# Attention's value products with 32 columns of weights, placed behind the scan's products by the list scheduler

## The chip, the cores and the metric

The kernel runs on one core of one Trainium2 chip. The metric is the device time of one execution in microseconds (us), as the median of several executions. Lower is better.

## The reference

One layer of a streaming encoder, 512 frames of 1024 columns, float32. Two token mixers work on the same input and are merged by gates. The change lies where the two mixers are computed side by side: the scan of the one (a delta rule) and the softmax attention of the other.

```python
x = x + 0.5 * swiglu(rms_norm(x, ffn1_norm), ffn1_w1, ffn1_w3, ffn1_w2)
h = rms_norm(x, mix_norm);  p = h @ w_in
# mixer A, 8 heads of 64, one step per frame
sa = einsum('bhvk,bhk->bhv', state, a_t)
state = state * w_t + sa * b_t^T + v_t * k_t^T
y_t = einsum('bhvk,bhk->bhv', state, r_t)
# mixer B, 8 heads of 64, blocks of 128 queries
s = einsum('bhqd,bhkd->bhqk', q_i, k) * scale + c_i[:, None] - cum[None, :]   # masked: s <= t
o = einsum('bhqk,bhkd->bhqd', softmax(s), v)                                  # "the values"
x = x + (sigmoid(g_A) * y_A + sigmoid(g_B) * y_B) @ w_out
x = x + 0.5 * swiglu(rms_norm(x, ffn2_norm), ffn2_w1, ffn2_w3, ffn2_w2)
out = rms_norm(x, final_norm)
```

## The kernel before, in words

Almost all matrix products are done three times over with split operands (a high and a low part), in a full 128x128 array. They fill the time before and after the stage that matters here.

In the stage of the change the kernel cuts the 512 frames into 16 chunks of 32 for the scan. One chunk is a chain over three engines: `product_x` (TensorE, tile `xps`), `copy_x` (VectorE, `Xs`), `product_u` (TensorE, `ups`), `copy_u` (ScalarE, into `RD`), `products_sy` (TensorE, `sps` for the state and `yps` for the output), `scale_s` (VectorE, back into `RD`), and then the next chunk's `product_x`. The products of `xps`, `sps` and `yps` use 32 columns of weights each, at one of four places (columns 0, 32, 64, 96 of the array). Those of `ups` use 64 rows and 64 columns, at one of two places. Before every second chunk `stage` transposes values (`vp`) and keys (`bp`), and every fourth chunk ends in transposes `yt`.

Around this chain the attention of four pairs of heads is computed (`Pair`, and `Block` for one or two blocks of 128 queries of a pair: three such objects for each pair, twelve in all). A `Block` makes its logits (`lp<-kb,qa` and `lp<-klc,qb`, full array), their maxima (VectorE), exponentials (ScalarE, tile `pts`) and division (VectorE), transposes them (`lp<-ident,pts`, full array), copies them to `tr` (ScalarE), and multiplies the values with them in `values` (`lp<-tr,vt`). In the kernel before, `values` uses 64 columns of weights for each of the two heads of a pair, at columns 0 and 64.

What is left of the time on TensorE is filled with columns of the input projection (`pq`, `pgt`: full array, 512 columns at a time, one third of a step being one instruction).

The order is made by a list scheduler, the class `Plan`, when the program is built. Every operation is entered by `op` with an engine, an estimated duration, what it depends on, a rank (SCAN before SIDE, NEXT, ROWS, FILL), buffers that it takes and frees (`takes`, `frees`: `tr` and `pf` are those of the attention's transposed weights and of its PSUM banks) and, on TensorE, a kind: `w` full-array products, `t` transposes, `m` products of 32 columns, `u` those of `ups`, and in the kernel before `n` for the values. `start` says when an operation could begin: after its dependencies, plus a margin (`lag`, `ahead`). `run` takes the operation that can begin first; of several, the one with the longest way behind it, with a bonus for a transposition behind `m`, `n` or `u`. `SWITCH` adds a price for a change of kind. The engines' queues then run in that order, each strictly in turn; whoever is not ready makes the rest of its queue wait. The queues of SyncE and GpSimd (loads and saves) are put in order by the framework.

Of the kernel before, what the change touches and what calls it, by code (L numbers as in the profile page):

```python
# [18 lines left out]
P = 128  # L19
# [6 lines left out]
NP = DA // P  # L26
C = 32
# [23 lines left out]
def kernel(  # L51
# [24 lines left out]
    dve, act, pe = [Queued(e, False) for e in (nc.vector, nc.scalar, nc.tensor)]  # L76
# [95 lines left out]
    SCAN, SIDE, NEXT, ROWS, FILL = range(5)  # L172

    def on(do, *a):
        return lambda: do(*a)

    class Plan:
# [9 lines left out]
        def op(s, engine, us, do, *deps, rank=0, takes=(), frees=(), later=0.0, kind="w"):  # L187
            s.ops.append(dict(engine=engine, us=us, do=do, deps=deps, rank=rank, takes=takes, frees=frees, later=later,
                              kind=kind, end=None, way=0.0))
            return s.ops[-1]  # L190

        def start(s, o):
            to, now = o["engine"], s.idle.get(o["engine"], 0.0)
            ahead = 0.0 if to != "PE" else 0.57 if o["rank"] == SCAN else 0.26 if o["rank"] == SIDE and o["kind"] in "tw" else 0.31
            for d in o["deps"]:
                if d["end"] is None:
                    return None
                by = d["engine"]
                lag = 0.32 if by == "PE" else 0.15 if by == to else 0.21
                now = max(now, d["end"] + (0.0 if by == to == "PE" else lag + ahead))  # L200
            for name in set(o["takes"]):
                n = sum(t == name for t in o["takes"])
                if len(s.room[name]) < n:
                    return None
                now = max(now, sorted(s.room[name])[n - 1])
            return now

        def run(s):
            todo = list(s.ops)
            for o in s.ops[::-1]:  # L210
                o["way"] = o["way"] + o["us"] if o["rank"] != FILL else 0.0
                for d in o["deps"]:
                    d["way"] = max(d["way"], o["way"] + 0.3)
            while todo:
                at = {n: now for n, o in enumerate(todo) for now in [s.start(o)] if now is not None}

                def first(n):
                    o = todo[n]
                    turn = o["engine"] == "PE" and o["kind"] == "t" and s.kind in "mnu"
                    return at[n], -o["way"] - (40.0 if turn else 0.0), n  # L220

                n = min(at, key=first)
                o = todo[n]
                if o["engine"] in ("DVE", "ACT") and o["rank"] != SCAN:
                    until = at[n] + 0.98 * o["us"]
                    n = next((m for m in at if todo[m]["engine"] == o["engine"] and todo[m]["rank"] == SCAN
                              and at[m] < until), n)
                o = todo.pop(n)
                us = o["us"]
                if o["engine"] == "PE":  # L230
                    change = "".join("n" if k in "mnu" else k for k in (s.kind, o["kind"]))
                    us += s.SWITCH.get(change, 0.0) if s.kind != o["kind"] else 0.0
                    s.kind = o["kind"]
                s.idle[o["engine"]] = at[n] + us
                o["end"] = at[n] + us + o["later"]
                for name in o["takes"]:
                    s.room[name].remove(min(s.room[name]))
                for name in o["frees"]:
                    s.room[name].append(o["end"] + 0.33)
                if o["do"]:  # L240
                    o["do"]()

# [810 lines left out]
    op = o1.enter_context(tc.tile_pool(name="o1", bufs=1, side="right"))  # L1053
# [37 lines left out]
    with ExitStack() as mx:  # L1091
# [284 lines left out]
        for t in range(C - 1):  # L1376
            n, m = t + 1, C - 1 - t
# [4 lines left out]
        tw = nc.scalar.dma_start(Td[:], TT)  # L1382
        Tb = Tall[:].rearrange("p (a c t) -> p a c t", a=2, c=NC)
        tv = Td[:].rearrange("(q i u) s t -> q i s u t", q=2, i=2)
        for i in range(2):
            for q in range(2):
                o = i * 64 + q * C
# [3 lines left out]
        def heads():  # L1391
            return [(p, q) for p in range(NP) for q in range(2)]

        def half(q):
            return slice(q * 64, (q + 1) * 64)
# [54 lines left out]
        vt = []  # L1450
# [8 lines left out]
        for b in range(NB):  # L1459
            o = vtp.tile([P, T], F32, name=f"vt{b}", tag=f"vt{b}")  # L1460
# [19 lines left out]
        at = b1.go(range(2))  # L1480
# [9 lines left out]
        at = b1.go(range(2, 5), a0.sum(at))  # L1490
        a1.out()
        b0.high()
        ahead = Gate(NP + 2)
        at = b1.go(range(5, 7), b0.sum(at))
# [5 lines left out]
        for q in range(2):  # L1500
            o = (1 - q) * 64
# [9 lines left out]
        at = ahead.go(range(7))  # L1511
        gate_out, ahead = ahead.out, ahead.go(range(7, KD), b1.sum(at))
        for q in range(2):
            o = (1 - q) * 64
# [7 lines left out]
        for q in range(2):  # L1522
            pool.memset(Rs[0][half(q), :, q, :], 0.0)
            for i in range(4):
                o = (1 - q) * 64
# [5 lines left out]
        op = plan.op  # L1531
        summed, gone = [op("SP", 0.0, None, later=us, frees=frees) for us, frees in ((3.0, ()), (3.5, ["w"]))]
        o = op("ACT", 0.69, b1.log, summed, rank=SCAN, takes=["t"], frees=["pf"])
        o = op("ACT", 0.63, b1.root, o, rank=SCAN)
# [33 lines left out]

        def product_x(c):
            Y["x"] = xps = pr.tile([P, 2, 64], F32, tag="b", name="xps")  # L1570
            for p, q in heads()[::-1]:
                o = (p // 2) * 64 + q * C
                pe.matmul(xps[o:o + C, p % 2, :], G[p][q][:, c, 0, :], Rs[c % 4][:, p, q, :], start=True, stop=True,
                          tile_position=(0, o))
# [4 lines left out]

        def product_u(c):  # L1580
            Y["u"] = ups = pr.tile([P, 2, 64], F32, tag="b", name="ups")
            for p in range(NP):
                h = half(p // 2)
                pe.matmul(ups[h, p % 2, :], Tb[h, p % 2, c, :], Y["Xs"][h, p % 2, :], start=True, stop=True)

# [135 lines left out]
        for m in range(NP + 3, 2 * KD):  # L1721
            g = Held()
            w, o = columns("pgt", COL_GA + m * P)
# [11 lines left out]
            o = op("DVE", 0.61, result, o, rank=NEXT, takes=["gs"], frees=["pm"])  # L1735
            if m + 1 < 2 * KD:
                o = op("ACT", 0.54 if tanhs else 1.82, opened, o, *roots, rank=ROWS)
# [47 lines left out]
        class Block:  # L1785
# [46 lines left out]
            def values(s):  # L1832
                for j, b in enumerate(s.bl):
                    for k in range(b + 1):
                        o = s.at[b] + k * P
                        for q in range(2):
                            h = 2 * s.pair.p + q
                            pe.matmul(s.lp[1][half(q), j * P:(j + 1) * P], vt[k][:, h * 64:(h + 1) * 64],
                                      s.tr[q][:, o:o + P], start=k == 0, stop=k == b)

            def copy_o(s):
                dve.tensor_copy(s.pair.qp[:, s.bl[0] * P:(s.bl[-1] + 1) * P], s.lp[1][:, 0:len(s.bl) * P])
# [1 line left out]
            def enter(s, operands):  # L1844
                for q in range(2):
                    us = sum(0.455 * (b + 1) * P / T + 0.02 for b in s.bl)
                    sees.append(op("PE", us, on(s.logits, q), *operands[q], rank=SIDE, takes=["pf"]))
                lit = sees[-2:]
                for q in range(2):
                    o = []  # L1850
                    for b in s.bl:
                        n = (b + 1) * P
                        e = op("DVE", 0.18 + 1.05e-3 * n, on(s.maximum, q, b), lit[q], rank=SIDE)
                        o.append(op("ACT", 0.26 + 0.83e-3 * n, on(s.exp, q, b), e, *turned[q][-1:], rank=SIDE))
                    exps.extend(o)
                    us = 0.16 + sum(0.13 + 0.69e-3 * (b + 1) * P for b in s.bl)
                    o = op("DVE", us, on(s.divide, q), *o, rank=SIDE)
                    lit[q] = op("PE", 0.11 * s.w / P, on(s.turn, q), o, rank=SIDE, kind="t")
                for q in range(2):
                    turned[q].append(lit[q])  # L1860
                o = [op("ACT", 0.1 + 0.75e-3 * s.w, on(s.copy_t, q), lit[q], *copies[-1:], rank=SIDE, takes=["tr"],
                        frees=["pf"] * (1 - q)) for q in range(2)]
                copies.append(o[1])
                us = 0.22 * sum(b + 1 for b in s.bl)
                o = op("PE", us, s.values, *o, rank=SIDE, frees=["tr"] * 2, kind="n")
                return op("DVE", 0.13 + 0.55e-3 * len(s.bl) * P, s.copy_o, o, rank=SIDE, frees=["pf"])

        outs = []
# [19 lines left out]
        o = []  # L1888
        for p in range(NP):
            o = op("ACT", 0.63, on(part_y, p), *outs[p], *sees, *o, rank=FILL)  # L1890
            o = [op("DVE", 0.69, on(part_l, p), o, rank=FILL)]
# [292 lines left out]
```

## Time and profile before

| | |
|---|---|
| runs shown | 1098.98, 1097.88, 1099.1 us; median 1098.98 us |
| profiled execution | 1097.66 us, of which the profile's span covers 1095.8 us |
| granted TensorE clock | 0.998 |
| TensorE busy | 99% of the span |
| VectorE, ScalarE, GpSimd busy | 76%, 61%, 19% |
| stage with the scan and the attention | from about 516 to 649 us of the span |

Times of lines are the start in us from the beginning of the span and the duration in us. A line joins instructions of one form that follow each other (x12). A matmul's own duration includes its way through the array, so several overlap; the distance from one line's start to the next line's start is what it holds the queue for. A float32 product stands as two records, a float32r product or a transposition as one.

### The profile page before, as it was taken

The numbers are of one execution on the slowest core, as the hardware profiler recorded it, in microseconds if no ns is written. First come the engines' busy times: TensorE is split into PE (matmuls) and PEld (weight loads), VectorE is DVE, ScalarE is ACT, GpSimd is POOL, SyncE is SP. The second block draws the span as 40 slices with busy tenths as digits, with TensorE's granted clock in tenths as the row PEclk, the third lists the DMA queues.
The fourth block names the chain that finished last, engine by engine and source line by source line (L and its number), as shares of the span: only waits on it lengthen the run. The fifth ranks groups of instructions, "written<-read, shape, count | busy, mean of one in ns | idle before, by whom it ended". The sixth has DMA issues, their size and how long they took to land.

```text
span 1095.8 us, 16697 instructions
## 1 busy us (share of the span) xinstructions
PE 1087.1 (99%) x6306; PEld 887.4 (81%) x6306; DVE 837.8 (76%) x1162; ACT 670.1 (61%) x1050; POOL 212.5 (19%) x255
## 2 busy tenths in 40 slices
PE   9999999999999999999999999999999999999997
PEld 7888888888887888888777777888888888888886
DVE  7997676789756699788877766877697766689874
ACT  6765556575554755346988856534576565576554
POOL 1211220134204112401000030112311202114210
PEclk9999999999999999999999999999999999999999
DMA  7989887879936434444112252645968888859972
GB/s 225 250 174 235 198 178 202 192 143 191 231 98 184 114 94 128 114 136 116 50 41 84 81 200 88 189 118 172 271 153 192 189 215 174 184 158 203 236 187 77
DMA packets 139725, 177.11 MB, mean 162 GB/s; under 512 B 9726, under 2 KB 75838, under 8 KB 139646
## 3 DMA queue, kind: packets, MB, share of 16 engines
q0 software_dynamic: 33328, 70.40, 33.7%
q1 hardware_dynamic: 105582, 104.21, 31.1%
q10 hardware_dynamic: 736, 1.45, 0.3%
q8 instruction: 50, 0.82, 0.3%
q14 instruction: 29, 0.24, 0.1%
HBM read 163.51 MB, written 12.52 MB: 161 GB/s over the span
## 4 chain that ended last, share of the span: by engine, by line
PE 97%; ACT 2%; DVE 1%; issue 0%; DVEq 0%; ACTq 0%
PE P L71 39%; PE P L145 5%; PE P L144 5%; PE P L143 5%; PE pgt L71 5%; PE lp L71 3%; PE pq L71 2%; PE ppj L71 2%; PE pk L145 2%; PE pk L143 2%; PE pk L144 2%; PE pb L71 2%; PE pa L71 1%; PE pw L144 1%; PE pw L145 1%; PE pw L143 1%
## 5 line engine op out<-in xcount | busy, mean ns | idle before, releaser
L71 PE MATMUL P<-sraw,q 128*128 128x512 f32 x344 | 91.3, 389 | 0.0
L135 ACT CAST whi<-raw 128x1024 fp32r<-128x1024 f32 (+3 forms) x43 | 41.1, 956 | 65.8 <-issue 19.3
L71 PEld LDWEIGHTS P<-sraw,q 128*128 128x128 f32 x344 | 64.6, 188 | 13.4
L71 PE MATMUL P<-swhi,q 128*128 128x512 f32 x224 | 71.4, 390 | 0.0
L71 PE MATMUL P<-sraw,wxh 128*128 128x512 f32 x200 | 68.4, 394 | 0.0
L136 DVE TENSOR_TENSOR wlo<-raw,whi 128x1024 fp32r<-128x1024 f32 (+3 forms) x44 | 49.6, 1127 | 16.3 <-ACT whi L135 15.2
L71 PE MATMUL P<-swhi,wxh 128*128 128x512 f32 x144 | 56.9, 395 | 0.0
L71 PE MATMUL P<-swhi,wxl 128*128 128x512 f32 x144 | 56.1, 390 | 0.0
L71 PE MATMUL P<-swlo,wxh 128*128 128x512 f32 x144 | 56.1, 389 | 0.0
L704 POOL DMA_DIRECT2D cb<-in_ffn_w_dram x20 | 24.1, 1204 | 150.1 <-DVE cd L71 85.3
L71 PE MATMUL P<-sraw,wxl 128*128 128x512 f32 x136 | 53.0, 390 | 0.0
L704 POOL DMA_DIRECT2D cd<-in_ffn_w_dram x24 | 29.5, 1229 | 102.6 <-DVE swlo L71 38.7
L71 PEld LDWEIGHTS P<-swhi,q 128*128 128x128 f32 x224 | 42.0, 188 | 8.7
L71 PE MATMUL P<-swlo,q 128*128 128x512 f32 x112 | 43.6, 389 | 0.0
L71 PEld LDWEIGHTS P<-sraw,wxh 128*128 128x128 f32 x200 | 37.2, 188 | 7.3
L71 ACT CAST sraw<-cd 128x1024 fp32r<-128x1024 f32 x30 | 31.5, 1050 | 15.1 <-PE P L71 11.5
L71 DVE TENSOR_TENSOR swlo<-ca,swhi 128x1024 fp32r<-128x1024 f32 x24 | 29.2, 1222 | 14.0 <-ACT swhi L71 14.0
L71 DVE TENSOR_TENSOR swlo<-cc,swhi 128x1024 fp32r<-128x1024 f32 x20 | 24.5, 1224 | 19.0 <-ACT swhi L71 18.7
L71 DVE TENSOR_TENSOR u<-P,u 128x512 f32<-128x512 f32 x52 | 34.1, 684 | 5.8 <-ACT u L71 5.7
L563 POOL DMA_DIRECT2D ca<-in_ffn_w_dram x16 | 19.3, 1205 | 96.2 <-DVE swlo L71 66.4
L143 PE MATMUL pk<-xh,whi 128*128 128x512 f32 x96 | 37.8, 394 | 0.0
L145 PE MATMUL pk<-xh,wlo 128*128 128x512 f32 x96 | 37.5, 391 | 0.2 <-DVE wlo L136 0.2
(616 smaller groups left out, 3446.9 us busy)
## 6 DMA issues: line engine op xcount, KB each, us to landing
raw<-in_w_in_dram SPq DMA_DIRECT2D x40, 512.0 KB
cc<-in_ffn_w_dram SPq DMA_DIRECT2D x36, 512.0 KB
cb<-in_ffn_w_dram POOLq DMA_DIRECT2D x36, 512.0 KB, 6.1
cb<-in_ffn_w_dram SPq DMA_DIRECT2D x32, 512.0 KB
cd<-in_ffn_w_dram POOLq DMA_DIRECT2D x32, 512.0 KB, 7.5
ca<-in_ffn_w_dram POOLq DMA_DIRECT2D x32, 512.0 KB, 7.6
ca<-in_ffn_w_dram SPq DMA_DIRECT2D x20, 512.0 KB
cd<-in_ffn_w_dram SPq DMA_DIRECT2D x18, 512.0 KB
```

Source lines behind the costliest of these rows:

```text
L71: q.last = do(*a, **kw)
L135: (hi_eng or act).copy(hi[:], raw[:])
L136: (eng or dve).tensor_tensor(lo[:], raw[:], hi[:].bitcast(F32), op=ALU.subtract)
L143: pe.matmul(ps, whi, xhi, start=first, stop=False, skip_group_check=onto)
L144: pe.matmul(ps, whi, xlo, start=False, stop=False, skip_group_check=onto)
L145: return pe.matmul(ps, wlo, xhi, start=False, stop=last, skip_group_check=onto)
L563: nc.gpsimd.dma_start(s.sum[g], src, accum_op=ALU.add)
L704: nc.gpsimd.dma_start(to, s.block(b, n, h), accum_op=ALU.add)
```

## The change

`values` now uses 32 columns of weights for each product, so four products take the place of two, at columns 0, 32, 64 and 96, each with the same 128 columns of moving operand as before. Its kind becomes `m`, like the scan's products. In the scheduler a value block that is not put behind a product of kind `m` is held back by 1.61 us more, and one that can follow such a product gets a bonus of 200 over the others that could begin at the same time. Margins and the bonus for transpositions get other numbers. `product_x` goes round four places instead of two by two, and `product_u` alternates between its two places.

```diff
-            ahead = 0.0 if to != "PE" else 0.57 if o["rank"] == SCAN else 0.26 if o["rank"] == SIDE and o["kind"] in "tw" else 0.31
+            ahead = 0.0 if to != "PE" else 0.75 if o["rank"] == SCAN else 0.27 if o["rank"] == SIDE else 0.36
+            ahead += 1.61 if o["kind"] == "m" != s.kind and o["rank"] != SCAN else 0.0
...
-                lag = 0.32 if by == "PE" else 0.15 if by == to else 0.21
+                lag = 0.28 if by == "PE" else 0.15 if by == to else 0.15
...
-                    turn = o["engine"] == "PE" and o["kind"] == "t" and s.kind in "mnu"
-                    return at[n], -o["way"] - (40.0 if turn else 0.0), n
+                    turn = o["engine"] == "PE" and o["kind"] == "t" and s.kind in "mu"
+                    same = o["kind"] == s.kind == "m"
+                    return at[n], -o["way"] - (10.0 if turn else 200.0 if same else 0.0), n
...
-                    until = at[n] + 0.98 * o["us"]
+                    until = at[n] + 1.11 * o["us"]
...
-                    s.room[name].append(o["end"] + 0.33)
+                    s.room[name].append(o["end"] + 0.35)
...
-            for p, q in heads()[::-1]:
+            for p, q in ((3, 1), (1, 1), (3, 0), (1, 0), (2, 1), (0, 1), (2, 0), (0, 0)):
...
-            for p in range(NP):
+            for p in (0, 2, 1, 3):
...
-                        for q in range(2):
-                            h = 2 * s.pair.p + q
-                            pe.matmul(s.lp[1][half(q), j * P:(j + 1) * P], vt[k][:, h * 64:(h + 1) * 64],
-                                      s.tr[q][:, o:o + P], start=k == 0, stop=k == b)
+                        for m in range(0, P, C):
+                            h = s.pair.p * P + m
+                            pe.matmul(s.lp[1][m:m + C, j * P:(j + 1) * P], vt[k][:, h:h + C],
+                                      s.tr[m // 64][:, o:o + P], start=k == 0, stop=k == b, tile_position=(0, m))
...
-                o = op("PE", us, s.values, *o, rank=SIDE, frees=["tr"] * 2, kind="n")
+                o = op("PE", us, s.values, *o, rank=SIDE, frees=["tr"] * 2, kind="m")
```

The order on TensorE, first place: the second value block (`lp<-tr,vt`), near the end of the fourth chunk, in the kernel before. `yps` ends the chunk's scan products, `pq` is filling work, `yt` are the transpositions of the scan's output.

```order
L71 MATMUL yps<-RD_4157,G_2539 32x64
L71 MATMUL pq<-xh_2444,whi 128x512
L71 MATMUL pq<-xl_2445,whi 128x512
L71 MATMUL pq<-xh_2444,wlo 128x512
L71 MATMUL lp<-tr,vt_3853 64x128 x2
L71 MATMUL lp<-tr,vt_3855 64x128 x2
L71 MATMUL lp<-tr,vt_3857 64x128 x2
L71 MATMUL yt<-ident,BK_2546 128x128
```

The same block on TensorE in the changed kernel.

```order
L71 MATMUL yps<-RD_4157,G_2539 32x64
L71 MATMUL lp<-tr,vt_3853 32x128 x4
L71 MATMUL lp<-tr,vt_3855 32x128 x4
L71 MATMUL lp<-tr,vt_3857 32x128 x4
L71 MATMUL lp<-ident,pts 128x128 x8
L71 MATMUL yt<-ident,BK_2546 128x128
```

The filling work between the scan's products and the values is gone from here; it stands elsewhere in the queue. The values are twice as many products of half the columns.

Second place, TensorE from the second chunk's `yps` to the third chunk's `ups`, in the kernel before. `lp<-ident,pts` transposes the weights of one head, `lp<-kb` and `lp<-klc` are logits of a later block.

```order
L71 MATMUL yps<-RD_4156,G_2539 32x64
L71 MATMUL pq<-xh_2593,whi 128x512
...
L71 MATMUL lp<-ident,pts 128x128 x3
...
L71 MATMUL xps<-RD_4157,G_2538 32x64
L71 MATMUL lp<-kb_4206,qa_4258 128x384
L71 MATMUL lp<-klc_3934,qb_4184 128x384
L71 MATMUL lp<-tr,vt_3853 64x128 x4
L71 MATMUL lp<-tr,vt_3855 64x128 x2
L71 MATMUL ups<-Xs,Tall 64x64 x4
```

The same stretch in the changed kernel.

```order
L71 MATMUL yps<-RD_4156,G_2539 32x64
L71 MATMUL lp<-ident,pts 128x128 x3
L71 MATMUL pq<-xh_2593,whi 128x512
...
L71 MATMUL lp<-kb_4206,qa_4261 128x384
L71 MATMUL lp<-klc_3934,qb_4184 128x384
...
L71 MATMUL xps<-RD_4157,G_2538 32x64
L71 MATMUL lp<-tr,vt_3853 32x128 x8
L71 MATMUL lp<-tr,vt_3855 32x128 x4
L71 MATMUL pq<-xh_2444,whi 128x512
...
L71 MATMUL ups<-Xs,Tall 64x64 x4
```

The values moved up to stand directly behind `xps`, the transpositions moved up to stand directly behind `yps` (three filling products less between them), and the logits moved ahead of `xps`.

Third place, SyncE's queue of loads at the end of the stage, in the kernel before. `G<-bsave` and `G<-lgsave` overwrite tiles that the scan's last `yps` read; `raw` are weights.

```order
L128 DMA raw<-in_w_in_dram 128x8x128 x4
L128 DMA raw<-in_fox_proj_dram 128x4x128
L1917 DMA G_2544<-bsave 128x512
L1915 DMA G_2543<-lgsave 96x512
L1917 DMA G_2545<-bsave 128x512
L128 DMA raw<-in_fox_proj_dram 128x4x128 x7
```

The same in the changed kernel.

```order
L128 DMA raw<-in_w_in_dram 128x8x128 x3
L128 DMA raw<-in_fox_proj_dram 128x4x128 x2
L1919 DMA G_2544<-bsave 128x512
L1917 DMA G_2543<-lgsave 96x512
L1919 DMA G_2545<-bsave 128x512
L128 DMA raw<-in_fox_proj_dram 128x4x128 x6
```

One load of weights has moved ahead of an earlier group of such loads, and one more stands before the three that wait for the scan.

Over the stage the twelve value blocks stand on TensorE so. Before: two between full-array products on both sides (the third and the twelfth), four between such products and transpositions (the second, fifth, ninth and tenth), six with a scan product (`xps`, `sps` or `ups`) directly before or behind them. After: eleven directly before or behind products of kind `m`, one (the third) between full-array products. The number of filling products, logits and transpositions is the same; 48 filling products stand behind the last `yt`, where 63 stood.

More of the change, by code (lines that the diff above doesn't have):

```diff
@@ L230, in run @@
                 if o["engine"] == "PE":
-                    change = "".join("n" if k in "mnu" else k for k in (s.kind, o["kind"]))
+                    change = "".join("n" if k in "mu" else k for k in (s.kind, o["kind"]))
                     us += s.SWITCH.get(change, 0.0) if s.kind != o["kind"] else 0.0
```

## The prediction

> **What bounds the kernel now.** I read the page's first part and its chain first, to see which engine sets the end.
>
> ```profile
> span 1095.8 us, 16697 instructions
> PE 1087.1 (99%) x6306; PEld 887.4 (81%) x6306; DVE 837.8 (76%) x1162; ACT 670.1 (61%) x1050; POOL 212.5 (19%) x255
> PE 97%; ACT 2%; DVE 1%; issue 0%; DVEq 0%; ACTq 0%
> ```
>
> TensorE (PE) is busy for 99% of the span and is 97% of the chain that ended last. Next, the busy time by stretches, with the stage of the change (516 to 649 us) and the tail behind it.
>
> ```profile
> 516.00:649.00 133.00, 132.44 (x1762) 99.71 (x1761) 101.18 (x256) 110.29 (x291) 9.78 (x18) 1.00 0.27 79
> 649.00:663.00 14.00, 14.00 (x65) 11.64 (x63) 2.61 (x3) 5.28 (x7) 3.20 (x7) 1.00 0.73 232
> ```
>
> The first number behind the length is PE: 132.44 of 133.00 us, at a granted clock of 1.00. VectorE (101.18) and ScalarE (110.29) have a quarter and a sixth of the stage to spare. The view of waits, for PE in this stage, has two entries alone:
>
> ```profile
> PE bp L71 <- ACT BK L71: 0.3, 1, 0.3
> PE lp L71 <- ACT tr L71: 0.3, 1, 0.3
> ```
>
> So the scan's chain over three engines does not set the pace. PE does, by what its queue holds: filling work covers the chain's latencies, and some of it is left over behind the scan. A microsecond taken from PE's queue here is a microsecond off the end, unless a wait takes its place. What can be taken is not arithmetic (the same columns stream through the array) but what a change of the array's shape costs. That cost is not shown as idle time; it is in the distances between starts.
>
> **The price of a change of shape.** The timeline of PE around the second and the third value block:
>
> ```profile
> 546.46 0.39 PE L71 MATMUL pq<-xh,wlo 128*128 128x512 f32 x1
> 546.77 0.65 PE L71 MATMUL sps<-RD,RD 128*32 128x64 f32 x32
> 547.25 0.41 PE L71 MATMUL yps<-RD,G 128*32 128x64 f32 x16
> 547.58 0.50 PE L71 MATMUL pq<-xh,whi 128*128 128x512 f32 x1
> 547.92 0.40 PE L71 MATMUL pq<-xl,whi 128*128 128x512 f32 x1
> 548.16 0.40 PE L71 MATMUL pq<-xh,wlo 128*128 128x512 f32 x1
> 548.49 0.88 PE L71 MATMUL lp<-tr,vt 128*64 128x128 f32 x12
> 549.29 0.66 PE L71 MATMUL yt<-ident,BK 128*128 128x128 f32 x4
> ...
> 553.48 1.09 PE L71 MATMUL lp<-tr,vt 128*64 128x128 f32 x16
> 554.50 0.50 PE L71 MATMUL pq<-xh,whi 128*128 128x512 f32 x1
> 554.84 0.40 PE L71 MATMUL pq<-xl,whi 128*128 128x512 f32 x1
> ```
>
> A value block of 12 records holds PE for 549.29 - 548.49 = 0.80 us, one of 16 for 554.50 - 553.48 = 1.02. Four records are 0.22, so one is 0.055 and the streams themselves are 0.66 and 0.88; the remaining 0.15 of each block is getting into and out of its shape. The neighbours pay too. A full-array product takes 548.16 - 547.92 = 0.24 among its like, 548.49 - 548.16 = 0.33 ahead of the values, and 0.34 as the first behind a change (547.58 to 547.92, 554.50 to 554.84): 0.09 to leave the full array, 0.10 to come back. A transposition group coming back pays less:
>
> ```profile
> 567.30 0.55 PE L71 MATMUL lp<-ident,pts 128*128 128x128 f32 x3
> 567.60 0.42 PE L71 MATMUL lp<-kb,qa 128*128 128x384 f32 x1
> ...
> 590.42 0.49 PE L71 MATMUL lp<-ident,pts 128*128 128x128 f32 x3
> 590.66 0.48 PE L71 MATMUL pgt<-xh,whi 128*128 128x512 f32 x1
> ```
>
> Behind scan products the three take 0.30, among full-array work 0.24: 0.06. A block at a scan product pays the 0.15 alone, whichever shape the neighbour has, as the seventh shows between `xps` and `pgt`, at 600.84 - 600.03 = 0.81:
>
> ```profile
> 599.66 0.44 PE L71 MATMUL xps<-RD,G 128*32 128x64 f32 x16
> 600.03 0.88 PE L71 MATMUL lp<-tr,vt 128*64 128x128 f32 x12
> 600.84 0.50 PE L71 MATMUL pgt<-xh,whi 128*128 128x512 f32 x1
> 601.73 0.46 PE L71 MATMUL ups<-Xs,Tall 64*64 64x64 f32 x8
> 602.12 0.45 PE L71 MATMUL lp<-kb,qa 128*128 128x384 f32 x1
> ```
>
> **The change part by part.** *Changes of shape.* By the order of before, two blocks stand between full-array products, worth 0.15 + 0.09 + 0.10 = 0.34 each; four between products and transpositions, 0.15 + 0.09 + 0.06 = 0.30; six at a scan product, 0.15. Together 0.68 + 1.20 + 0.90 = 2.78 us. In the changed order eleven stand at a product of the same shape and pay nothing of their own: the way out of the shape is the one that the scan product paid anyway. The third still stands between `pq` products: -0.34. The gain is 2.44 us.
>
> *Four products of 32 columns for two of 64.* No row shows this. From one side: each place streams as many columns as before and four run where two ran, so a block keeps its 0.66 or 0.88. From the other, the 32 records of `sps`, of that shape with 64 columns, hold PE for 547.25 - 546.77 = 0.47, or 0.0147 each; 24 and 32 records of twice the columns are then 0.71 and 0.94, dearer by 0.05 in eight blocks and by 0.06 in four: 0.6 us. That includes coming into the shape, which a value block behind a scan product does not pay, so I take 0 and keep 0.6 as the end. Cheaper than before it can't be at the same column rate.
>
> *`product_x` round four places.* `xps` takes 600.03 - 599.66 = 0.37, `yps` with as many records round four places 547.58 - 547.25 = 0.33. At most 16 x 0.04 = 0.6 is in it; but `yps` follows `sps` in the same shape and `xps` comes from another, which explains part of it. I take 0.2, with ends 0 and 0.6. *`product_u` alternating.* Eight records take 602.12 - 601.73 = 0.39 with their ends. By `sps` a record is 4 x 0.0147 = 0.059 at one place; one after the other eight would take 0.47, so the two places run side by side already. I take 0.
>
> *Waits that the new order brings.* The place with the tightest rows is the second of the order's, behind the second chunk:
>
> ```profile
> 531.44 0.42 PE L71 MATMUL yps<-RD,G 128*32 128x64 f32 x16
> 532.59 0.49 PE L71 MATMUL lp<-ident,pts 128*128 128x128 f32 x3
> 533.71 0.44 PE L71 MATMUL xps<-RD,G 128*32 128x64 f32 x16
> 534.42 0.44 PE L71 MATMUL lp<-kb,qa 128*128 128x384 f32 x1 [0.27 <-ACT tr L71]
> ...
> 531.94 0.42 DVE L71 TENSOR_SCALAR pts<-pts,mx 128x384 f32<-128x384 f32 x1
> ```
>
> The transpositions read `pts` that VectorE has divided by 531.94 + 0.42 = 532.36. They now stand directly behind `yps`; in the timing of before PE would be there at 531.44 + 0.33 = 531.77 and wait 0.6. Three filling products have moved ahead of `sps` here, 3 x 0.24 = 0.7 us, so PE comes later and the wait is anything from 0 to 0.6. Behind a waiting transposition stand the third chunk's `xps` and the whole scan, but the filling left over behind the scan means that only the wait itself is lost. The logits `lp<-kb`, which waited 0.27 for ScalarE's copy of the same transpositions, stand three filling products behind them as before, and will wait about as long. Eleven more such joints exist. I put the waits at one of these more than before, +0.35, with ends of -0.3 (the present one goes) and +1.0 (three come).
>
> *What costs nothing.* The filling behind the last `yt` shrinks from 63 products to 48, about 11 us. It covers the last block's way through VectorE and ScalarE and the loads that wait for the scan:
>
> ```profile
> 645.49 0.29 DVE L71 COPY qk<-lp 128x128 f32<-128x128 f32 x1 [0.92 <-PE lp L71]
> 646.92 0.68 DVE L71 TENSOR_TENSOR yl<-qk,yh 128x512 fp32r<-128x512 f32 x1
> ...
> 663.47 1.02 PE L71 MATMUL yc<-V,center 128*128 128x512 f32 x2
> ...
> 646.53 0.34 SPq L1917 DMA_DIRECT2D G<-bsave  x1
> 648.76 0.38 SPq L128 DMA_DIRECT2D raw<-in_fox_proj_dram  x1
> ```
>
> From the last values' copy to the end of its split are 646.92 + 0.68 - 645.49 = 2.1 us, so 11 us hide it. On SyncE the second `raw<-in_fox_proj` moves ahead of the `G` loads; it went out 2.2 us behind them, so it can hold them up by some 2 us, and they too have 11. If that cover were gone, the first products behind the tail would pay the difference.
>
> *Sum.* -2.44 - 0.2 + 0 + 0 + 0.35 = -2.3 us. The profiled execution (1097.66 us, of which 1095.8 are the span) would come to 1095.4; it stands 1.3 below the median of the runs, 1098.98, from which the same 2.3 makes 1096.7. A measurement of this kernel tells about 0.2%, 2.2 us, from no change, so this forecast lies just at that edge. Its own range, with the ends above (saving 2.44 + 0.6 + 0.3 = 3.3 at best, 2.44 - 0.6 - 1.0 = 0.8 at worst, and not all ends together), is 1096.0 to 1097.8.
>
> **The rivals.** *The gain comes back as waits.* A value block held back keeps its `tr` and `pf` buffers for longer, so copies and logits of the next block come later, and transpositions that took the first place behind `yps` meet a division that is not done. For it: the wait of 0.27 above is of just this kind. Against it: ScalarE and VectorE have room, and the scheduler moves filling in front of what is not ready. If every second of the twelve blocks brings a wait of 0.3, 1.8 us are lost, and with 2.64 saved by the rest the time is 1098.98 - 2.64 + 1.8 = 1098.1. Chance 0.20.
>
> *More than forecast.* If the waits of before go (two of 0.3 by the view of waits) and no new ones come, and `xps` gives its 0.6: 2.44 + 0.6 + 0.6 = 3.6, 1095.3. For it: the new margins are wider towards the scan. Chance 0.13.
>
> *Slower: weight loads come into the open.* Twice as many weights are loaded. The rows of loads:
>
> ```profile
> L71 PEld LDWEIGHTS sps<-RD,RD x480: 106/110/110, 525.2 to 638.8; 128*32 128x32 f32 x160
> L71 PEld LDWEIGHTS lp<-tr,vt x160: 132/137/137, 535.0 to 645.0; 128*64 128x64 f32 x160
> ```
>
> A load of 32 columns takes 110 ns by itself, one of 64 columns 137. The 160 records in twelve blocks become 320, four at a time in 80 rounds. If each round shows one load of 0.11 us, 8.8 us are added, and with the other terms the time is 1098.98 - 2.3 + 8.8 = 1105.5; it decides from 21 open rounds (2.3 us) on. Against it speak the `sps` rows themselves: 32 records of the same shape in 0.47 us, 0.0147 each, can't hold a load of 0.11 for each or for each four (8 rounds x 0.11 = 0.88). The Trainium skill (TensorE: Matmul & The Clock Gate, Part 3, The mechanism) says that a weight load overlaps with running products only when its row group differs, and all four places here share all rows; by that rule this rival would hold. The trace disagrees with it, by the 0.47 us for 32 records. Chance 0.07.
>
> **How the numbers follow.** Forecast 0.60, gain lost to waits 0.20, more than forecast 0.13, slower 0.07. Faster by over 0.2% is below 1096.8: all of the third case and 0.42 of the forecast's 0.60 (its point lies just past the edge, and of its unknown costs the four places and the alternation have no row that speaks for a loss): 0.55. Slower by over 0.2%: 0.07. Within: 0.38. The range takes the forecast with its ends, most of the third case and most of the waits' case: 1095.2 to 1098.7.
>
> **What would show it.** In the changed profile: value lines in the form 128*32 with x24 and x32, at a distance of 0.65 to 0.7 and 0.88 to 0.94 between a scan product and what follows, plus 0.1 where they leave the shape; 0.28 instead of 0.37 for an `xps` with values behind it; `xps` by itself at 0.34 to 0.37; PE waits in the stage of about 0.6 to 1.3 in all. The first product behind the tail (`yc`, now at 663.47) should start 2 to 2.5 us earlier, and everything behind it by the same. Values of 24 records that hold PE for over 0.9 us would make the slower rival right; values at 0.66 with `yc` less than 1 us earlier, the waits.

## The result and the profile after

The changed kernel takes 1095.95 us (median, 1095.78 to 1096.62), the kernel before, run beside it, 1098.51 us (1097.79 to 1099.1). The ratio is 0.9979 with a 95% interval of 0.9971 to 0.9987: faster by 2.56 us by the medians. The profiled executions differ by 1095.8 - 1093.6 = 2.2 us of span.

The first part and the chain of the changed kernel's page:

```profile
span 1093.6 us, 17021 instructions
PE 1084.8 (99%) x6466; PEld 886.4 (81%) x6466; DVE 837.2 (77%) x1162; ACT 669.1 (61%) x1050; POOL 212.4 (19%) x255
PE 96%; DVE 2%; ACT 1%; issue 0%; DVEq 0%; ACTq 0%
```

TensorE has 160 records more and is busy for 2.3 us less. It is still what bounds the kernel. The busy time by the same two stretches as before:

```profile
516.00:649.00 133.00, 132.18 (x1924) 100.75 (x1926) 99.23 (x254) 109.33 (x290) 8.85 (x17) 1.00 0.28 80
649.00:663.00 14.00, 14.00 (x75) 10.99 (x68) 5.44 (x9) 7.13 (x11) 4.07 (x8) 1.00 0.69 221
```

The stage looks as full as before (132.18 for 132.44): what was saved is filled with other products, and shows only where the queue runs out. So the ruler for this study is the stretch from the first `vp` (the stage's first scan instruction) to the first `yc` (the first product behind the tail), both on TensorE. Between them stand in all kernels here the same 384 full-array products, 160 transpositions, 496 products of `xps`, `sps` and `yps` and 64 of `ups`, and the same values (80 products of 64 columns or 160 of 32). The two ends, in the timeline of before (its `yc` is shown above, at 663.47):

```profile
516.22 0.60 PE L71 MATMUL vp<-ident,V 128*64 128x128 f32 x4
```

and of the changed kernel:

```profile
516.44 0.60 PE L71 MATMUL vp<-ident,V 128*64 128x128 f32 x4
661.50 2.73 PE L71 MATMUL yc<-V,center 128*128 128x512 f32 x6
```

663.47 - 516.22 = 147.25 before, 661.50 - 516.44 = 145.06 after: 2.19 us less. Behind the first `yc` the spans run on for 432.3 and 432.1 us. The stage began 0.2 us later here; in a second profile of the same changed program it began 0.6 us later still, and the stretch was 145.04. So the start varies by more than half a microsecond between executions, and the stretch repeats to 0.02. The 2.56 of the medians is 0.37 more than the stretch shows; the medians of the kernel before alone lie between 1098.06 and 1098.51 in the four groups of runs here.

Value blocks in the changed kernel's timeline, behind `xps`, behind `yps`, ahead of `sps`, and the third block, which still stands among `pq`:

```profile
535.47 0.43 PE L71 MATMUL xps<-RD,G 128*32 128x64 f32 x16
535.72 0.84 PE L71 MATMUL lp<-tr,vt 128*32 128x128 f32 x24
536.49 0.50 PE L71 MATMUL pq<-xh,whi 128*128 128x512 f32 x1
...
549.57 0.41 PE L71 MATMUL yps<-RD,G 128*32 128x64 f32 x16
549.79 0.84 PE L71 MATMUL lp<-tr,vt 128*32 128x128 f32 x24
550.56 1.09 PE L71 MATMUL lp<-ident,pts 128*128 128x128 f32 x8
...
555.44 1.08 PE L71 MATMUL lp<-tr,vt 128*32 128x128 f32 x32
556.45 0.50 PE L71 MATMUL pq<-xh,whi 128*128 128x512 f32 x1
...
580.69 0.86 PE L71 MATMUL lp<-tr,vt 128*32 128x128 f32 x24
581.37 0.63 PE L71 MATMUL sps<-RD,RD 128*32 128x64 f32 x32
581.81 0.40 PE L71 MATMUL yps<-RD,G 128*32 128x64 f32 x15
```

The scan product hands over after 0.25 us (`xps`) or 0.22 (`yps`), where it took 0.37 or 0.33 with another shape behind it in the kernel before; the values then hold PE for 0.77. Blocks of 32 records in the same place hold it for 0.99 (the sixth, 591.13 - 590.14), so eight records are 0.22, the stream of 24 is 0.66, and 0.11 is the way out of the shape. Ahead of `sps` a block takes 0.68 and `sps` itself 0.44 for 0.47. The block among full-array products takes 1.01 for 1.02 before.

The view of waits for PE in the stage:

```profile
PE lp L71 <- DVE pts L71: 0.5, 1, 0.5
PE bp L71 <- ACT BK L71: 0.3, 1, 0.3
```

The wait for `tr` has gone, and the one behind the second chunk's `yps` has come. PE's timeline has the place:

```profile
532.34 0.41 PE L71 MATMUL yps<-RD,G 128*32 128x64 f32 x16
533.22 0.52 PE L71 MATMUL lp<-ident,pts 128*128 128x128 f32 x3 [0.47 <-DVE pts L71]
...
617.65 0.40 PE L71 MATMUL pgt<-xh,wlo 128*128 128x512 f32 x1
618.08 0.33 PE L71 MATMUL lp<-kb,qa 128*128 128x128 f32 x1
...
617.44 0.59 ACT L71 COPY tr<-lp 128x512 f32<-128x512 f32 x1
```

The last two lines of PE are a wait that the view leaves out: 0.43 pass from a full-array product to a logit, where 0.23 or 0.24 pass from one full-array product to the next. ScalarE's copy to `tr` ends at 617.44 + 0.59 = 618.03, just ahead of that logit.

### The profile page after: what moved, and what is told of

Its sections match the earlier page's. It is cut to its first block, busy times and chain, and to the rows that moved or that the text cites. A ratio compares the mean times of both kernels' runs of the same rounds, so it can differ in the third digit from the quotient of the medians.

```text
span 1093.6 us, 17021 instructions
## 1 busy us (share of the span) xinstructions
PE 1084.8 (99%) x6466; PEld 886.4 (81%) x6466; DVE 837.2 (77%) x1162; ACT 669.1 (61%) x1050; POOL 212.4 (19%) x255
## 4 chain that ended last, share of the span: by engine, by line
PE 96%; DVE 2%; ACT 1%; issue 0%; DVEq 0%; ACTq 0%
PE P L71 39%; PE P L143 5%; PE P L145 5%; PE P L144 5%; PE pgt L71 5%; PE lp L71 3%; PE pq L71 2%; PE ppj L71 2%; PE pk L145 2%; PE pk L144 2%; PE pk L143 2%; PE pb L71 2%; PE pa L71 1%; PE pw L144 1%; PE pw L143 1%; PE pw L145 1%
```

## The experiments

Each kernel was timed beside the kernel before on the same chip, whose medians there were 1098.06 (first four), 1098.10 (next four) and 1098.33 (last three). The stretch is that of one profiled execution. In three of these rows (the orders alone, the 64 columns, the margins alone) the interval of the ratio takes in 1, and in two more it ends at 0.9999, so what these five show rests on the stretch and on the distances in it, not on the time.

| kernel | stretch, us | against before | median, us | ratio to before (95%) |
|---|---|---|---|---|
| before | 147.25 | | 1098.51 | |
| changed | 145.06 | -2.19 | 1095.95 | 0.9979 (0.9971 to 0.9987) |
| orders of `xps` and `ups` alone | 146.99 | -0.26 | 1098.18 | 1.0002 (0.9992 to 1.0011) |
| changed order, 64 columns | 146.57 | -0.68 | 1097.51 | 0.9992 (0.9984 to 1.0001) |
| order of before, 32 columns | 146.60 | -0.65 | 1097.12 | 0.9991 (0.9982 to 0.9999) |
| margins alone | 147.50 | +0.25 | 1098.91 | 1.0005 (0.9997 to 1.0014) |
| no hold, no bonus | 145.82 | -1.43 | 1097.11 | 0.9990 (0.9981 to 0.9999) |
| margin 0.26 | 144.26 | -2.99 | 1095.25 | 0.9974 (0.9963 to 0.9984) |
| margin 0.26 and 1.0 | 143.92 | -3.33 | 1094.88 | 0.9970 (0.9959 to 0.9982) |
| hold 2.0 | 148.04 | +0.79 | 1100.23 | 1.0020 (1.0011 to 1.0029) |
| hold 2.0, margin 0.26 | 144.84 | -2.41 | 1095.49 | 0.9975 (0.9966 to 0.9984) |
| changed, again | 145.04 | -2.21 | 1095.90 | 0.9980 (0.9971 to 0.9990) |
| margin 0.26 and 1.0, again | 143.93 | -3.32 | 1094.79 | 0.9970 (0.9958 to 0.9982) |

**The orders of `product_x` and `product_u` alone.**

```diff
-            for p, q in heads()[::-1]:
+            for p, q in ((3, 1), (1, 1), (3, 0), (1, 0), (2, 1), (0, 1), (2, 0), (0, 0)):
...
-            for p in range(NP):
+            for p in (0, 2, 1, 3):
```

> The kernel before with one part of the change alone: product_x goes round four places, product_u alternates; the order on TensorE is otherwise that of before. By the step of the prediction: -0.2 us in all (ends 0 and -0.6). From the distances in the changed kernel, where an xps with full-array work on both sides fell from 0.375 to 0.361 us and a ups from 0.385 to 0.378: 16 x 0.014 + 16 x 0.007 = 0.3 us less than before. Rival: those short distances come from what stands around them there, and the orders by themselves give nothing: xps stays at 0.375, ups at 0.385. The time alone can hardly tell 0.3 us; the distances decide.

The same rows of its timeline as those of before in the prediction:

```profile
599.68 0.43 PE L71 MATMUL xps<-RD,G 128*32 128x64 f32 x16
600.04 0.88 PE L71 MATMUL lp<-tr,vt 128*64 128x128 f32 x12
...
601.74 0.45 PE L71 MATMUL ups<-Xs,Tall 64*64 64x64 f32 x8
602.12 0.45 PE L71 MATMUL lp<-kb,qa 128*128 128x384 f32 x1
```

Unrounded, `xps` takes 0.361 (0.374 before) and `ups` 0.378 (0.385), the same as in the changed kernel, so the orders do it and not the neighbours. The stretch is 0.26 shorter; the two waits of the kernel before are there too, each 0.02 longer. The time can't show it, as expected: the interval reaches 0.9 us below and 1.2 above no change.

**The changed order with 64 columns.** The order on TensorE is the changed kernel's, product group for product group.

```diff
-                        for m in range(0, P, C):
-                            h = s.pair.p * P + m
-                            pe.matmul(s.lp[1][m:m + C, j * P:(j + 1) * P], vt[k][:, h:h + C],
-                                      s.tr[m // 64][:, o:o + P], start=k == 0, stop=k == b, tile_position=(0, m))
+                        for q in range(2):
+                            h = 2 * s.pair.p + q
+                            pe.matmul(s.lp[1][half(q), j * P:(j + 1) * P], vt[k][:, h * 64:(h + 1) * 64],
+                                      s.tr[q][:, o:o + P], start=k == 0, stop=k == b)
```

> The changed kernel with its order, kinds and margins kept, but each value product with 64 columns of weights again (two places). Only the shape is undone. Theory: the gain is the shape; eleven blocks pay 0.15 to 0.16 us each again, 1.7 us, so the time is 1.7 over the changed kernel and 0.9 under the kernel before (ratio to before 0.9992). An xps or yps with values behind it goes back from 0.25 and 0.22 us to about 0.37 and 0.33. Rival 1: the gain is the order alone (fewer waits, other filling work at the end): within 0.4 us of the changed kernel, ratio 0.998. Rival 2: the order brings nothing without the shape, and the wait of 0.5 behind the second chunk stays: 0 to 0.5 us over the kernel before.

The fourth block in its timeline:

```profile
568.14 0.43 PE L71 MATMUL xps<-RD,G 128*32 128x64 f32 x16
568.50 0.88 PE L71 MATMUL lp<-tr,vt 128*64 128x128 f32 x12
569.31 0.50 PE L71 MATMUL pgt<-xh,whi 128*128 128x512 f32 x1
...
618.49 0.40 PE L71 MATMUL pgt<-xh,wlo 128*128 128x512 f32 x1
618.76 0.33 PE L71 MATMUL lp<-kb,qa 128*128 128x128 f32 x1
```

The pair of `xps` and values takes 0.36 + 0.81 = 1.17 where the changed kernel has 0.25 + 0.77 = 1.02: the 0.15 of the forecast, for each of the eleven blocks 1.65 in all. The stretch is 146.57 - 145.06 = 1.51 longer than the changed kernel's; the last two rows say where the rest is. They take 0.27 here and 0.43 in the changed kernel: whose PE comes to that logit earlier, and waits 0.16 there. 1.65 - 0.16 = 1.49. Both rivals fail: the order alone, with its waits, brings 0.68 - 0.26 = 0.42 us, not 2 and not nothing.

**The order of before with 32 columns.** The same lines of `values` in the other direction, in the kernel before.

> The kernel before with its order kept, but the value products with 32 columns of weights (four places). Theory: five of the twelve blocks stand at a product of xps or sps and lose 0.15 us each, the other seven change nothing: 0.75 us under the kernel before. Blocks between full-array products still take about 0.77 to 0.81 for 24 records and 0.99 to 1.02 for 32. Rival 1: four products of 32 columns cost more than two of 64 (the sps rate, 0.0147 a record): twelve blocks dearer by 0.05, 0.6 in all, so only 0.15 is left. Rival 2, the slower one: each round of four shows a weight load of 0.11 us, 80 rounds: 8 us over.

A block ahead of `yt` and one behind `xps`, in its timeline:

```profile
548.51 0.86 PE L71 MATMUL lp<-tr,vt 128*32 128x128 f32 x24
549.31 0.66 PE L71 MATMUL yt<-ident,BK 128*128 128x128 f32 x4
...
599.38 0.44 PE L71 MATMUL xps<-RD,G 128*32 128x64 f32 x16
599.62 0.85 PE L71 MATMUL lp<-tr,vt 128*32 128x128 f32 x24
600.41 0.50 PE L71 MATMUL pgt<-xh,whi 128*128 128x512 f32 x1
```

Away from a scan product 24 records take 0.80, as the 12 of 64 columns did (unrounded 0.794 for 0.806); behind `xps` the pair takes 0.24 + 0.79 = 1.03. Four products of 32 columns cost no more than two of 64, and no weight load shows. The stretch is 0.65 shorter (0.75 expected). This refutes the slower rival by itself: the shape without the order is no loss.

**The margins alone.**

```diff
-            ahead = 0.0 if to != "PE" else 0.57 if o["rank"] == SCAN else 0.26 if o["rank"] == SIDE and o["kind"] in "tw" else 0.31
+            ahead = 0.0 if to != "PE" else 0.75 if o["rank"] == SCAN else 0.27 if o["rank"] == SIDE else 0.36
...
-                lag = 0.32 if by == "PE" else 0.15 if by == to else 0.21
+                lag = 0.28 if by == "PE" else 0.15 if by == to else 0.15
...
-                    return at[n], -o["way"] - (40.0 if turn else 0.0), n
+                    return at[n], -o["way"] - (10.0 if turn else 0.0), n
...
-                    until = at[n] + 0.98 * o["us"]
+                    until = at[n] + 1.11 * o["us"]
...
-                    s.room[name].append(o["end"] + 0.33)
+                    s.room[name].append(o["end"] + 0.35)
```

> The kernel before with the scheduler's new margins (0.75, 0.27, 0.36, 0.28, 0.15, 1.11, 0.35) and the bonus of 10 alone: values of 64 columns and of their own kind, no hold of 1.61, no bonus of 200, the old orders of product_x and product_u. In this order seven blocks stand at a scan product (0.15 each), three between full-array products (0.34), two with transpositions (0.30): 2.67 against 2.78, so 0.1 us less by shape changes, and the wait of some 0.5 behind the second chunk is there too. Theory: 0.4 us over the kernel before, so no gain. Rival: the margins carry the gain by taking waits away: 1 us or more under the kernel before.

Its waits of PE in the stage:

```profile
PE lp L71 <- DVE pts L71: 0.4, 1, 0.4
...
```

The other wait is that of 0.3 for `BK`, as before. The wait behind the second chunk is there without any of the rest, so it comes from the margins. They bring no gain: 0.25 us more stretch, ratio 1.0005.

**No hold, no bonus.** The changed kernel without the two rules that put values to scan products.

```diff
-            ahead += 1.61 if o["kind"] == "m" != s.kind and o["rank"] != SCAN else 0.0
...
-                    return at[n], -o["way"] - (10.0 if turn else 200.0 if same else 0.0), n
+                    return at[n], -o["way"] - (10.0 if turn else 0.0), n
```

> The changed kernel without the two rules that bring values to scan products: no hold of 1.61, no bonus of 200. Margins, kinds, 32 columns and the two orders stay. In its order six of the twelve blocks stand at an xps, yps or sps; the others stand at ups (three), between logits (one), and between transpositions or logits and other work (two). Theory: each of these six pays a change of shape again that the changed kernel doesn't: 0.15 at ups, 0.3 elsewhere; minus the one between full-array products that the changed kernel keeps (0.3). Together about 1 us over the changed kernel, 1.4 under the kernel before (ratio 0.9987). Rival: the 32 columns and the margins do it, and the place is of no matter: the same as the changed kernel (ratio 0.998). Other rival: the hold costs waits (blocks come later), so that without it the time is lower still.

The stretch is 0.76 longer than the changed kernel's, 1 expected; the ratio 0.9990. Six blocks still stand at scan products, though no rule asks for it here. The two rules are worth about a third of the change.

**The margin behind ScalarE and VectorE.**

```diff
-                lag = 0.28 if by == "PE" else 0.15 if by == to else 0.15
+                lag = 0.28 if by == "PE" else 0.15 if by == to else 0.26
```

> The changed kernel with one number of the scheduler changed: the margin behind ScalarE and VectorE 0.26 instead of 0.15. In its order six full-array products and a transposition stand between the second chunk's yps and the next lp<-ident,pts, so the wait of 0.5 for pts should be gone, and all twelve value blocks stand at a scan product or (two of them) behind ups. Theory: the wait was on the path, so 0.5 to 0.8 us less than the changed kernel (ratio to before 0.9973), with only 18 filling products behind the last yt (4 us), still enough. Rival: a wait that goes comes back elsewhere (18 instead of 48 products left over means that more filling stands in front of things that are ready): the same as the changed kernel or up to 1 us over.

The stretch is 0.80 shorter than the changed kernel's; the medians differ by 0.7. With one more number (`until = at[n] + 1.0 * o["us"]`):

> As the run with the margin 0.26, and the number that lets the scan's work go ahead on VectorE and ScalarE 1.0 instead of 1.11. The order differs from that run only behind the twelfth chunk. Theory: the same gain of 0.5 to 0.9 us against the changed kernel, since block places and the second chunk are the same. Rival: the last four chunks bring a wait (fewer fillings between xps and ups there): no better than the changed kernel.

Its waits of PE in the stage:

```profile
PE pgt L71 <- DVE gs L71: 0.4, 1, 0.4
```

Against the changed kernel three waits, of 0.5, 0.3 and 0.2 (the one that the view leaves out), have gone and one of 0.4 has come. All blocks stand at a scan product, the third behind `ups`. The stretch is 1.14 shorter. 0.6 of it are the waits; the rest was not taken apart.

**A longer hold.**

```diff
-            ahead += 1.61 if o["kind"] == "m" != s.kind and o["rank"] != SCAN else 0.0
+            ahead += 2.0 if o["kind"] == "m" != s.kind and o["rank"] != SCAN else 0.0
```

> The changed kernel with one number changed: the hold is 2.0 instead of 1.61. The eighth block then goes behind yps rather than before sps, eleven blocks still stand at scan products, but in the chunk that follows only three filling products are left between ups and sps, where the smallest distance in the changed kernel is 2.64 us: 0.38 + 0.1 + 3 x 0.23 = 1.2 us, while copy_u is done 0.50 + 1.08 = 1.6 us behind the ups at the earliest. Theory: the gain hangs on waits as much as on shapes; here PE waits 0.4 to 2 us more, and the time is that much over the changed kernel (ratio 0.998 to 1.000). Rival: the filling left over covers that too, and the time is the changed kernel's.

By the medians it is slower than the kernel before by 2.1 us and than the changed kernel by some 4. In the stretch it is 0.79 longer than the kernel before and 3.0 longer than the changed kernel, where 0.4 to 2 were expected. So over 1 us of the loss lies outside the stretch. The profiled execution (1099.46 us) began the stage 0.8 later than that of the kernel before and ran 0.3 longer behind `yc`; the eleven executions show granted clocks of 0.995 to 0.998, those of the kernel before beside them 0.998 or 0.999. Whether the waits lower the clock was not tested.

Its waits of PE in the stage, of which the last, 0.3 for `BK`, is as before:

```profile
PE lp L71 <- ACT tr L71: 1.6, 1, 1.6
PE sps L71 <- ACT RD L71: 0.6, 1, 0.6
PE lp L71 <- DVE pts L71: 0.5, 1, 0.5
...
```

And the timeline of PE there, then of ScalarE:

```profile
610.59 0.86 PE L71 MATMUL lp<-tr,vt 128*32 128x128 f32 x24
611.39 0.50 PE L71 MATMUL pgt<-xh,whi 128*128 128x512 f32 x1
...
614.23 0.45 PE L71 MATMUL ups<-Xs,Tall 64*64 64x64 f32 x8
...
616.14 0.87 PE L71 MATMUL sps<-RD,RD 128*32 128x64 f32 x30 [0.57 <-ACT RD L71]
616.80 0.25 PE L71 MATMUL yps<-RD,G 128*32 128x64 f32 x2
...
617.22 1.09 PE L71 MATMUL lp<-ident,pts 128*128 128x128 f32 x8
619.96 0.33 PE L71 MATMUL lp<-kb,qa 128*128 128x128 f32 x1 [1.64 <-ACT tr L71]
```

```profile
614.51 0.68 ACT L71 ACTIVATE pts<-lp,mx 128x512 f32<-128x512 f32 x1
...
615.30 1.07 ACT L71 COPY RD<-ups 32x128 f32<-32x128 f32 x4
616.28 1.24 ACT L71 CAST qb<-qk 64x512 fp32r<-64x512 f32 x2
617.55 1.05 ACT L71 CAST whi<-raw 128x1024 fp32r<-128x1024 f32 x1
618.50 0.62 ACT L71 ACTIVATE gs<-gs 128x512 f32<-128x512 f32 x1
619.15 0.27 ACT L71 COPY BK<-yps 128x128 f32<-128x128 f32 x1
619.31 1.08 ACT L71 COPY tr<-lp 128x512 f32<-128x512 f32 x2
```

The `sps` wait is of the kind expected (three products behind `ups`), and longer, since ScalarE was still at an exponential when `ups` was done. The larger one was not expected: logits stand directly behind transpositions whose copies to `tr` are queued on ScalarE behind two casts, an activation for a gate and the copy of `yps`, and start 619.31 - 617.22 = 2.1 us behind the transpositions. The expectation was also wrong on the order: ten blocks, not eleven, stand at scan products, and the eighth went among full-array products (the first two rows), worth about 0.3. With the 0.66 that 30 records of `sps` took instead of 0.44, and without the wait of 0.16 that the changed kernel has, the sum is 1.64 + 0.57 + 0.3 + 0.22 - 0.16 = 2.6 of the 3.0 us in the stretch.

**The longer hold with the wider margin.**

```diff
-            ahead += 1.61 if o["kind"] == "m" != s.kind and o["rank"] != SCAN else 0.0
+            ahead += 2.0 if o["kind"] == "m" != s.kind and o["rank"] != SCAN else 0.0
...
-                lag = 0.28 if by == "PE" else 0.15 if by == to else 0.15
+                lag = 0.28 if by == "PE" else 0.15 if by == to else 0.26
```

> The hold of 2.0 that cost 4 us, with the margin behind ScalarE and VectorE at 0.26 instead of 0.15. Theory: the time went to waits for ScalarE and VectorE that the order had not left room for, not to the hold as such; with the wider margin the waits of 1.6, 0.6 and 0.5 go, two blocks of twelve stand at no scan product (0.3 each), and the time is that of the margin 0.26 with the hold of 1.61 within 0.6 us (ratio to before 0.997 to 0.998). Rival: a longer hold delays the blocks themselves (their tr and pf buffers come free later), whatever the margin: 1 us or more over the kernel before again.

One wait is left in the view:

```profile
PE bp L71 <- DVE RD L71: 0.5, 1, 0.5
```

The loss of 4 us is gone, with the hold as long as it was: it came with waits that the order had left no room for, not with the hold as such. By itself the longer hold still costs a little: the stretch is 0.58 longer than with the hold of 1.61 and the same margin, within the expected 0.6.

**The changed kernel and the best version on one chip.**

> The changed kernel again, on the same chip as the two beside it, for a direct comparison: ratio to before 0.998, 2.2 to 2.6 us less.

> The version with the margin 0.26 and the number 1.0, on the same chip as the changed kernel. Theory: 0.9 to 1.3 us less than the changed kernel (its first yc came 1.3 us earlier), so a ratio of 0.997 to before. Rival: the 1.3 us were one execution's, and the two agree within 0.4 us.

1095.90 and 1094.79: the version with 0.26 and 1.0 is 1.1 us below the changed kernel, and its stretch is 1.11 shorter, in the second profile as in the first (1.14). The two ratios' intervals overlap; that both profiles and both medians agree is what speaks for it.

## Why the prediction was right

The mechanism held, and the saving nearly so: -2.3 us forecast, -2.19 in the stretch, -2.56 by the medians. The time of 1095.95 us lies inside the stated range and 0.05 below the forecast's own (1096.0 to 1097.8). Of the 0.75 between it and the forecast of 1096.7, 0.47 come from the base: the forecast starts at 1098.98, the median of three runs, and the twelve beside the result have 1098.51.

- *Changes of shape*, -2.44 forecast. Measured: 0.15 for each of eleven blocks in the place of the forecast, by the run with 64 columns (1.65 of its own, 1.51 less the new wait). What the order saves by taking blocks from between full-array products and transpositions was forecast as 2.78 - 0.34 - 1.65 = 0.79; the runs show 0.42 (146.99 - 146.57), and the 0.2 of waits that came with it make it 0.62. So this part is some 0.17 too large and the whole term about 2.3. What the missing 0.17 is stays open.
- *Four products of 32 columns for two of 64*, 0. Measured 0.01 less for a block away from the scan: 0.794 for 0.806, and 1.01 for 1.02. The end of +0.6 from the `sps` rate is refuted; that rate holds the way into the shape, as the prediction said: unrounded, `sps` takes 0.447 behind values and 0.471 elsewhere.
- *`product_x` and `product_u`*, -0.2 and 0. Measured -0.26 together by the stretch; the distances of one, 0.014 and 0.007, would make 0.34 in 16 chunks. The larger end, 0.6, was not reached, because `yps` is shorter than `xps` mostly by what stands ahead of it: the one `yps` of the kernel before that stands behind a full-array product takes 0.361, as `xps` does in the new order, and those behind `sps` take 0.337.
- *Waits*, +0.35. Measured: 0.5 came, 0.3 went, and 0.16 came at a logit, +0.36. The first is the one named, behind the second chunk, and stems from the margins, as the run with the margins alone shows. The prediction expected the logits `lp<-kb` of the third chunk to wait on; that wait went, and the one at another logit was not foreseen. So the place and the size of the first wait were read rightly, and that the sum comes out so well is luck.
- *Free edits.* The view of waits has none of PE behind the last `yt`, and from the first `yc` to the end of the span are 432.3 us before and 432.1 after, so neither the shorter tail nor SyncE's order cost anything.
- *The sum of the parts* -0.26, -0.42 and -0.65 is -1.33. The changed kernel has -2.19: in the order of before five of the twelve blocks stand where the new shape pays (at `xps` or `sps`), in the changed order eleven, and the six others get there only by the new order. By the stretch the shape is worth 0.65 in the old order and 1.51 in the new one.
- *The signs that it named.* Values that leave the shape hold PE for 0.77 and 0.99 (0.75 to 0.8 and 0.98 to 1.04 expected). An `xps` by itself takes 0.36 (0.34 to 0.37), with values behind it 0.25 instead of the expected 0.28: the way out of the 32-column shape is 0.11, and the prediction took the 0.09 of the full array. PE's waits are 0.5 + 0.3 + 0.16 = 0.96 in all (0.6 to 1.3). `yc` starts 1.97 earlier (2 to 2.5), 2.19 earlier when counted from the first `vp`.

*The rivals.* The slower one fell by the 0.80 us for 24 records, whose loads of 0.11 each would be 2.6 us one after the other. The rule of the Trainium skill (TensorE: Matmul & The Clock Gate, Part 3, The mechanism) that a load overlaps with running products only when its row group differs, taken alone, is not what these traces show. The gain given back as waits did not happen in this order, but it is near: with the hold of 2.0 ten blocks have the new shape at scan products, and the time ends 0.2% over the kernel before. The price of 1.8 us was of the right kind and too low for that order (2.2 in two new waits alone); the chance of 0.20 can't be judged by one result. The third case (3.6 us saved) is what the version with margin 0.26 and 1.0 comes near, with 3.3, though not in the way named: one new wait of 0.4 came, and the new orders of `xps` and `ups` gave 0.26, not 0.6.

## What to carry to other kernels

Where one engine's queue is full, idle time is no guide: measure the distance from start to start of unlike neighbours against like ones, and multiply by the joints (places where the shape changes) that the order has. A change of shape and a change of order can be worth more together than the sum of both, as here, where the shape pays only at neighbours of its own kind. And an order made by a scheduler must leave room for the queues of the other engines: here 0.39 us more in one number brought a single wait of 1.6 us, so read the waits of each new order before its time.

## What the runs showed of the hardware

- Between scan products and values of the same 32-column shape a change of product costs nothing: `xps` hands over to values after 0.25 us and to full-array products and transpositions after 0.36. Leaving the shape costs 0.11 us, whoever leaves it: 0.36 for 0.25 at `xps`, 0.34 for 0.22 at `yps`, 0.77 for the stream of 0.66 at values. Coming into it costs 0.02 (`sps` takes 0.471 behind other shapes and 0.447 behind values).
- Going round the four places with `xps`, instead of two and two, saves 0.014 us of 0.375 for its 16 records; alternating the two places of `ups` saves 0.007 of 0.385 for its eight.
- The same program began this stage up to 0.6 us apart in two executions (first `vp` at 516.44 and 517.07), with the stretch from there equal to 0.02 us. So a part of this program could be measured far better than its whole, since its two ends and the work between them are the same.
